# Two parked loads on another queue, and the returns of a norm tied behind the ways out

## The chip, the cores and the metric

The kernel runs on one core of one Trainium2 chip. The metric is the device time of one execution in microseconds; a lower number is better. Times of the kernel before are given as the median of three runs, and one further execution was taken with the hardware profiler.

## The reference

The program is a two-layer decoder trunk on 256 tokens of width 2048 in float32. Layer 0 mixes with gated linear attention, layer 1 with softmax attention that has a forget gate; both also attend to 256 memory tokens. Each layer ends in a gated MLP with a causal convolution of width 3. What matters here is the passage from layer 0 to layer 1:

```python
x = x + conv_ffn(rmsnorm(x, norm_ffn[0]), ...)        # end of layer 0
hs = rmsnorm(x, fox_kv_norm)                          # "kv" norm
k, v, fl = split_cols(hs @ fox_w_kv, [1536, 1536, 12])   # K and V of layer 1
mk, mv = memory_kv(mem_n, mem_w_kv[1])                # keys and values of the memory, layer 1
h = rmsnorm(x, norm_mix[1])                           # input of the queries of layer 1
```

So K and V of layer 1 need the whole of x after the last down projection of layer 0, normalised. The memory's keys and values of layer 1 don't depend on x, and they are first read when layer 1 attends to the memory.

## The kernel before

**Matrix products.** Every product is split into high and low float32r halves, and three of the four partial products are kept. A weight is streamed in units of at most 128 x 1024 (`raw`, four buffers), loaded on SP's queue (L224). ScalarE makes its high half (`whi`, L229) and VectorE its low half (`wlo`, L230), four buffers each. A panel of 512 columns that takes tokens as its rows (`panel_tm`, matmuls at L333) has eight units of two 128-row chunks, and 12 matmuls a unit: two chunks, two token blocks, high x high, high x low and low x high.

**The order of the work.** A planner fills each engine's queue from the order in which the program states things and from priorities (`high_priority`). Each engine then works through its own queue in that order; an instruction that waits holds all that stands behind it on the same engine, DMA issues included. `tc.issue_after(ins)` puts the instructions of its block behind `ins` where they share an engine, and adds no wait. The list `loads` holds the weight loads.

**Turning the residual.** x stands with tokens on partitions and is needed with features on partitions. A block `f` (0 to 3) is 512 features of all 256 tokens. For each block the norm's `then(f, b)` (in `preparing`) transposes 32 x 32 pieces on VectorE for both token halves `b` (L1592, into `blk` or `tblk`). After the second half, `far_away` sends the block to DRAM (the way out, L632, 512 KB, into `far`, three buffers). Later `land` calls `back`, which brings it back in four loads of 128 KB in another order (the return, L637, into `fvt` for blocks 0 to 2 and `fky` for block 3). Then `take` (`split_turned`, L524 on ScalarE for the high half, L526 on VectorE for the low half) scales it into `B` (chunks 4f to 4f+3), the input of K and V. The queries' input is made from the same block by the same two lines (`query_input`, out-tiles `mix` and `A`). For the "kv" norm at the end of layer 0 these transfers are issued by GpSimd (`queue=nc.gpsimd`); for the norms "ffn0" and "ffn1" they are issued by SP. In the MLP of layer 0, other blocks (`yu`) take the same way out and back on GpSimd.

**The end of layer 0.** The last down projections run as `wide` (blocks 0 and 1), `f2` (block 2) and `f3` (block 3). The program states `land()` of block 0 after unit 4 of `f2`, of block 1 after unit 5, of block 2 before unit 5 of `f3`; block 3 is landed inside layer 1's second K panel. Then `fox` starts with the K panels 0 and 1: six units of panel 0, six of panel 1, then the last two of each.

**Parked memory.** Layer 1's memory keys and values (`mk[1]`, `mv[1]`, 512 KB each) are computed early. The MLP of layer 0 needs their room for the hidden activations (`moremk`, `moremv`), so both are written to DRAM before it (`parked`, on GpSimd) and loaded back once the last matmul that reads the room is done (L1203, `mk1again` and `mv1again`). The program states that load in `fox`, in the second of four V panels after its fourth unit. They are read by `mem_parts(1, "B")` (L668, L669) after the last V panel.

Of the kernel before, what the change touches and what calls it, by code (L numbers as in the profile page):

```python
# [21 lines left out]
T = 256  # L22
# [123 lines left out]
def _trunk(ctx: ExitStack, tc: tile.TileContext, xt, xtok, memt, wp, wgu, gns, gfin, cnv, par, msk, out):  # L146
    nc = tc.nc
# [37 lines left out]
        for i in range(WARM):  # L185
            TE.matmul(warm, bufB[KC - 1][:, 0, :P], bufB[KC - 1], start=i == 0, stop=i == WARM - 1)

    loads, casts, lows, ends, last_mm = [], [], [], [], []
    scratch = [sm]
    parked = []  # L190

# [120 lines left out]
    def panel_tm(key, src, evac, second=False):  # L312

        units = where[key]
        n = units[0][2]
        base = min(min(u[1]) for u in units)
        acc = []
        end = len(units) - 1  # L320

        def step(i):
            if i == 0:
                acc.extend(work("s", 2) if second else pacc.tile([P, 512], F32, name="acc", tag="acc")
                           for _ in range(2))
            ready = split_unit(units[i])
            passes = [(b, low) for low in range(2) for b in range(2)]
            if i == end:
                passes.sort()
            for b, low in passes:  # L330
                for j, kc in enumerate(units[i][1]):
                    for part in range(2 - low):
                        mm = TE.matmul(acc[b][:, :n], src[kc - base][:, part, b * P : (b + 1) * P],  # L333
                                       ready[low][:, j * n : (j + 1) * n], start=i == low == part == j == 0,
                                       stop=i == end and low == 1 and j == len(units[i][1]) - 1)
                if i == end and low:
                    ends.append(mm)
                    evac(b, acc[b][:, :n])
            last_mm.append(mm)

        return step
# [177 lines left out]
    def split_turned(dst, i, z, name):  # L519

        g = gain(name, i)
        hi, lo = (dst[i][:, part, :].rearrange("p (b q j) -> p b q j", b=2, q=4) for part in range(2))
        src = z[:, :, i % 4].rearrange("p q b j -> p b q j")
        S.activation(hi, src, AF.Copy, scale=g)  # L524
        for b in range(2):
            V.scalar_tensor_tensor(lo[:, b], src[:, b], g, hi[:, b].bitcast(F32), ALU.mult, ALU.subtract)  # L526
# [102 lines left out]
    def far_away(pool, src, n, queue=nc.sync):  # L629

        far = pool.tile([P, 4 * T], F32, name="far", tag="far", bufs=3)
        queue.dma_start(far[:, : 4 * n], src[:, : 4 * n])  # L632
        blocks = far[:, : 4 * n].rearrange("(q i) (c n) -> c i q n", q=4, c=4)

        def back(dst):
            for c in range(4):
                queue.dma_start(dst[32 * c : 32 * (c + 1), : 4 * n].rearrange("i (q n) -> i q n", q=4), blocks[c])  # L637

        return back

    def move_far(pool, dst, src, n):
        far_away(pool, src, n)(dst)

    def flat(t):
        return t.rearrange("p c k b j -> p (c k b j)")
# [8 lines left out]
    def turn_out(y, done):  # L654

        def evac(b, a):
            with tc.high_priority(offset=AHEAD):
                V.transpose(y[:, :, :, b, :], a.rearrange("p (k c i) -> p c k i", c=4, i=32))
            if b:
                done(far_away(dram, flat(y), T))  # L660

        return evac
# [468 lines left out]
    def fox(nx, vt, stash):  # L1131
        hk, hq, mix = bufB, bufA, bufB
        with (
# [16 lines left out]
            def keys():  # L1150
                j, back, z = open_.pop(0)
                with tc.issue_after(loads[-1].ins):
                    back(flat(z))
                with tc.issue_after(lows[-1].ins):
                    for k in range(4):
                        V.tensor_tensor(by_run(kt[:, 4 * j + k, :]), z[:, :, k], by_run(nx.row()), ALU.mult)

            def query_input(i):
                split_turned(hq, i, (*stash, spare[1])[i // 4], "mix1")
# [11 lines left out]
            def forget():  # L1171
                fl = turn()
                bias = part[:, C_BF : C_BF + 1]
                e = fp.tile([P, T], F32, name="fe", tag="tmp", bufs=5)
                S.activation(e, fl, AF.Abs, bias=bias)
                S.activation(e, e, AF.Exp, scale=-1.0)
                S.activation(e, e, AF.Ln, bias=1.0)
                mz = fp.tile([P, T], F32, name="fm", tag="tmp", bufs=5)
                V.tensor_scalar(mz, fl, bias, 0.0, ALU.add, ALU.min)
                V.tensor_tensor(mz, mz, e, ALU.subtract)  # L1180
                V.tensor_tensor_scan(cs, ones[:, 0:1].to_broadcast([P, T]), mz, 0.0, ALU.mult, ALU.add)
                pc = work("t")
                for b in range(2):
                    TE.transpose(pc[:, b * P : (b + 1) * P], cs[:, b * P : (b + 1) * P], ident)
                V.tensor_copy(cc, pc[:, :T].rearrange("p (b h) -> p b h", b=2)[:, :, :FOX_H])

            for j, (lo, hi) in enumerate(FV_PARTS):
                def fv_out(b, a, j=j, lo=lo, hi=hi):
                    S.activation(vt[:, b, lo:hi], a[:, : hi - lo], AF.Copy, scale=nx.col()[:, b : b + 1])
                    if j == 0:  # L1190
                        take(b, a[:, hi - lo :])
                        if b:
                            forget()

                step = panel_tm(("fv", j), hk, fv_out)
                for u in range(8):
                    step(u)
                    if (j, u) in ((0, 0), (0, 2), (1, 2)):
                        keys()
                    if (j, u) == (1, 3):  # L1200
                        for t, tag, far in ((mk, "mk1", parked[0]), (mv, "mv1", parked[1])):
                            t[1] = const.tile(list(t[1].shape), F32, name=tag + "again", tag=tag)
                            nc.gpsimd.dma_start(t[1].rearrange("p a b -> p (a b)"), far)  # L1203
                    if j == 0:
                        query_input(4 + u)

# [31 lines left out]
            def take(pair, head):  # L1238

                def evac(c, a):  # L1240
                    if c == 0 and pair >= BEHIND:
                        values(pair - BEHIND)
                    head(c, a)
                    if c:
                        move_far(dp, zs[pair % 3], ys[pair % 2], T if pair < 2 else 6 * 32)

                proj_fm(("mq", 1, pair) if pair < 2 else ("fq", pair - 2), hq, evac)
# [312 lines left out]
    def preparing(name, dst, pool, far, kept=None, tag="blk", queue=nc.sync):  # L1560

        n = StreamNorm()
        blocks, rooms, turned_blocks = {}, {}, []
        away, landed = [], []

        def land(z=None):  # L1570

            f, back = away.pop(0)
            if z is None:
                z = pool.tile([P, 4, 4, 2, 32], F32, name="turn", tag="turn", bufs=2) if kept is None else kept[f]
            with tc.issue_after(loads[-1].ins) if queue is nc.sync else nullcontext():
                back(flat(z))
            landed.append((f, z))

        def take():

            f, z = landed.pop(0)
            with tc.issue_after(casts[-1].ins):
                for k in range(4):
                    split_turned(dst, 4 * f + k, z, name)

        def then(f, b):
            n.add(f, b)
            with tc.high_priority(offset=AHEAD):
                if b == 0:
                    blocks[f] = rooms[f]() if f in rooms else pool.tile([P, 4, 4, 2, 32], F32, name="blk", tag=tag, bufs=2)  # L1590
                y = blocks[f]
                turned_blocks.append(V.transpose(y[:, :, :, b, :],  # L1592
                                                 x[f][:, b, :].rearrange("p (k c i) -> p c k i", c=4, i=32)))
                if b:
                    away.append((f, far_away(far, flat(y), T, queue)))

        n.rooms = then.rooms = rooms
        then.turned = turned_blocks
        n.land = then.land = land
        n.take = then.take = take  # L1600
        return n, then

    n = gla(nx)
# [20 lines left out]
    with tc.tile_pool(name="turn2", bufs=1) as tp:  # L1624
        n, then = preparing("ffn1", bufA, tp, dram)
# [137 lines left out]
```

## Time and profile before

| | us |
|---|---|
| median of 3 runs | 2244.25 |
| lowest, highest | 2242.79, 2245.59 |
| the profiled execution | 2243.66 |
| its span, first to last instruction | 2241.9 |

| engine | busy us | share of the span |
|---|---|---|
| TensorE, matmuls (PE) | 2216.0 | 99% |
| TensorE, weight loads (PEld) | 1855.5 | 83% |
| VectorE (DVE) | 1781.2 | 79% |
| ScalarE (ACT) | 1419.2 | 63% |
| GpSimd (POOL) | 137.1 | 6% |

The busy time of TensorE counts a matmul from its start to its modelled end; matmuls overlap, and a matmul that runs at a lower clock or follows the one before it late is busy all the same. So a share of 99% doesn't say that no time is lost. The profile names who ended each engine's idle time, gives the granted clock of TensorE in any stretch (1.00 is full), and the time from the issue of a DMA to its landing. Rows that begin with a number have the start in microseconds from the span's start. In DMA rows POOLq is GpSimd's queue and SPq is SP's; in SP's and GpSimd's timelines the length of a DMA row is that of its issue, not that of the transfer.

### The profile page before, as it was taken

The numbers are of one execution on the slowest core, as the hardware profiler recorded it, in microseconds if no ns is written. First come the engines' busy times: TensorE is split into PE (matmuls) and PEld (weight loads), VectorE is DVE, ScalarE is ACT, GpSimd is POOL, SyncE is SP. The second block draws the span as 40 slices with busy tenths as digits, with TensorE's granted clock in tenths as the row PEclk, the third lists the DMA queues.
The fourth block names the chain that finished last, engine by engine and source line by source line (L and its number), as shares of the span: only waits on it lengthen the run. The fifth ranks groups of instructions, "written<-read, shape, count | busy, mean of one in ns | idle before, by whom it ended". The sixth has DMA issues, their size and how long they took to land.

```text
span 2241.9 us, 30033 instructions
## 1 busy us (share of the span) xinstructions
PE 2216.0 (99%) x10323; PEld 1855.5 (83%) x10323; DVE 1781.2 (79%) x2638; ACT 1419.2 (63%) x2255; POOL 137.1 (6%) x259
## 2 busy tenths in 40 slices
PE   9999999999999999999989999999999999999998
PEld 7888888888788888888877998888878888888886
DVE  7768987688887889888867559768888788978876
ACT  6655665556886567674665455455788647676466
POOL 0000000001100001100111000000100000110010
PEclk9999999999999999999999999999999999999999
DMA  9867657877677667766776767777777757776674
GB/s 352 248 220 222 199 183 248 247 243 240 217 245 243 206 215 253 230 213 220 226 244 225 221 197 233 241 235 242 224 230 243 244 197 229 257 233 209 224 239 158
DMA packets 165633, 515.47 MB, mean 230 GB/s; under 512 B 20700, under 2 KB 41832, under 8 KB 165480
## 3 DMA queue, kind: packets, MB, share of 16 engines
q1 hardware_dynamic: 148200, 460.32, 63.4%
q0 software_dynamic: 16704, 52.44, 7.6%
q8 instruction: 81, 1.33, 0.2%
q10 hardware_dynamic: 576, 0.79, 0.1%
q14 instruction: 72, 0.59, 0.1%
HBM read 469.68 MB, written 43.79 MB: 229 GB/s over the span
## 4 chain that ended last, share of the span: by engine, by line
PE 83%; issue 7%; ACT 4%; DMA 3%; DVE 1%; POOL 1%; ACTq 0%; DVEq 0%; POOLq 0%
PE acc L400 25%; PE acc L333 23%; PE ps_s L400 12%; PE ps_o L400 6%; PE ps_t L400 6%; PE acc L305 3%; PE acc L260 3%; PE ps_s L333 2%; ACT tap L1379 2%; PE acc L258 1%; ACT whi L229 1%; DMA raw<-wp 1%; DMA yzu<-far 1%; DMA far<-tblk 1%; DMA fvt<-far 1%
## 5 line engine op out<-in xcount | busy, mean ns | idle before, releaser
L230 DVE TENSOR_TENSOR wlo<-raw,whi 128x1024 fp32r<-128x1024 f32 (+4 forms) x739 | 875.6, 1196 | 305.0 <-ACT whi L229 287.8
L229 ACT ACTIVATE whi<-raw 128x1024 fp32r<-128x1024 f32 (+4 forms) x739 | 761.4, 1037 | 454.2 <-PE acc L333 171.7
L333 PE MATMUL acc<-whi,B 128*128 128x512 f32 (+3 forms) x1248 | 296.9, 373 | 10.9 <-ACT B L524 8.5
L333 PEld LDWEIGHTS acc<-whi,B 128*128 128x128 f32 x1248 | 229.2, 190 | 40.7 <-ACT B L524 9.3
L375 ACT ACTIVATE whi<-raw 128x1024 fp32r<-128x1024 f32 (+1 forms) x136 | 129.9, 955 | 196.3 <-PE acc L400 71.8
L400 PE MATMUL acc<-whi,B 128*128 128x512 f32 x794 | 203.3, 390 | 1.5 <-ACT whi L229 1.3
L376 DVE TENSOR_TENSOR wlo<-raw,whi 128x1024 fp32r<-128x1024 f32 (+1 forms) x136 | 148.1, 1090 | 69.3 <-ACT whi L375 61.7
L400 PE MATMUL acc<-whi,mix 128*128 128x512 f32 x754 | 192.7, 390 | 1.3 <-ACT whi L229 1.1
L400 PEld LDWEIGHTS acc<-whi,B 128*128 128x128 f32 x794 | 148.6, 188 | 34.6 <-ACT whi L229 3.8
L400 PEld LDWEIGHTS acc<-whi,mix 128*128 128x128 f32 x754 | 141.3, 188 | 32.7 <-ACT whi L229 3.0
L333 PE MATMUL acc<-wlo,B 128*128 128x512 f32 (+3 forms) x624 | 160.9, 371 | 0.0
L1379 ACT ACTIVATE tap<-fvt,cw 128x256 f32<-128x256 f32 x264 | 124.4, 530 | 6.9 <-DMA fvt<-far 6.9
L333 PEld LDWEIGHTS acc<-wlo,B 128*128 128x128 f32 x624 | 115.5, 189 | 14.9
L1379 ACT ACTIVATE tap<-yzu,cw 128x256 f32<-128x256 f32 x264 | 124.6, 531 | 4.7 <-DMA yzu<-far 4.7
L1386 DVE TENSOR_TENSOR tap<-tap,tap 128x1024 f32<-128x1024 f32 x88 | 107.0, 1216 | 19.6 <-ACT tap L1379 19.6
L400 PE MATMUL acc<-wlo,B 128*128 128x512 f32 x397 | 112.4, 390 | 0.0
L400 PE MATMUL ps_s<-whi,mix 128*128 128x512 f32 x394 | 107.3, 390 | 0.0
L400 PE MATMUL acc<-wlo,mix 128*128 128x512 f32 x377 | 106.6, 390 | 0.0
L400 PE MATMUL ps_s<-whi,B 128*128 128x512 f32 x342 | 94.3, 390 | 0.0
L400 PEld LDWEIGHTS acc<-wlo,B 128*128 128x128 f32 x397 | 74.4, 188 | 15.9 <-DVE wlo L230 0.5
L400 PEld LDWEIGHTS ps_s<-whi,mix 128*128 128x128 f32 x394 | 74.0, 188 | 15.6
L400 PEld LDWEIGHTS acc<-wlo,mix 128*128 128x128 f32 x377 | 70.6, 188 | 15.2 <-DVE wlo L230 0.5
(492 smaller groups left out, 3759.9 us busy)
## 6 DMA issues: line engine op xcount, KB each, us to landing
raw<-wp SPq DMA_DIRECT2D x743, 512.0 KB, 4.6
fvt<-far POOLq DMA_DIRECT2D x100, 128.0 KB, 5.2
raw<-wp SPq DMA_DIRECT2D x32, 384.0 KB, 3.5
far<-yu POOLq DMA_DIRECT2D x22, 512.0 KB, 5.8
far<-yzu POOLq DMA_DIRECT2D x22, 512.0 KB, 5.8
yzu<-far POOLq DMA_DIRECT2D x88, 128.0 KB, 5.6
raw<-wp SPq DMA_DIRECT2D x24, 388.0 KB, 3.5
x<-xtok SPq DMA_DIRECT2D x8, 512.0 KB, 6.3
```

Source lines behind the costliest of these rows:

```text
L229: casts.append(S.activation(hi[:, s], raw[:, s], AF.Copy))
L230: lows.append(V.tensor_tensor(lo[:, s], raw[:, s], hi[:, s].bitcast(F32), ALU.subtract))
L258: mm = TE.matmul(acc[p][c][:, :T], w[:, s], both[:, 0, :], start=False, stop=end and j == 3)
L260: mm = TE.matmul(acc[p][c], w[:, s], both, start=u == j == 0, stop=end and j == 3)
L305: mm = TE.matmul(acc[b][:, :n], src[kcs[j] - base][:, part, b * P : (b + 1) * P], w, start=u == 0 and low == part == j == 0, stop=u == end ...
L333: mm = TE.matmul(acc[b][:, :n], src[kc - base][:, part, b * P : (b + 1) * P], ready[low][:, j * n : (j + 1) * n], start=i == low == part = ...
L375: casts.append(S.activation(hi[:, :n], src, AF.Copy))
L376: lows.append(V.tensor_tensor(lo[:, :n], src, hi[:, :n].bitcast(F32), ALU.subtract))
L400: r = TE.matmul(bank[name], x, w, start=name not in begun, stop=last)
L1379: S.activation(by_run(taps[i][:, s, c, i:]), zs[slot][:, :, 2 * c + s], AF.Copy if i else AF.Identity, bias=0.0 if i else w[3], scale=w[2 ...
L1386: V.tensor_tensor(taps[0], taps[0], taps[n][:, :, :, :T], ALU.add)
```

## The change

The two loads of the parked memory are issued by SP instead of GpSimd, and they stand behind the weight load that was stated last at that place of the program (a load of the second V panel). `far_away` keeps each way out and the last load of each return in a new list `sent`. For the norm whose transfers GpSimd issues, a return stands behind the last entry of `sent`, and so does a way out. In the order of the program this puts the return of block 0 behind the way out of block 1, the way out of block 2 behind the return of block 0, the return of block 1 behind the way out of block 2, the return of block 2 behind that of block 1, and the way out of block 3 behind the return of block 2.

```diff
-    loads, casts, lows, ends, last_mm = [], [], [], [], []
+    loads, casts, lows, ends, last_mm, sent = [], [], [], [], [], []
 ...
     def far_away(pool, src, n, queue=nc.sync):
 
         far = pool.tile([P, 4 * T], F32, name="far", tag="far", bufs=3)
-        queue.dma_start(far[:, : 4 * n], src[:, : 4 * n])
+        sent.append(queue.dma_start(far[:, : 4 * n], src[:, : 4 * n]))
         blocks = far[:, : 4 * n].rearrange("(q i) (c n) -> c i q n", q=4, c=4)
 
         def back(dst):
             for c in range(4):
-                queue.dma_start(dst[32 * c : 32 * (c + 1), : 4 * n].rearrange("i (q n) -> i q n", q=4), blocks[c])
+                last_one = queue.dma_start(dst[32 * c : 32 * (c + 1), : 4 * n].rearrange("i (q n) -> i q n", q=4), blocks[c])
+            sent.append(last_one)
 
         return back
 ...
                     if (j, u) == (1, 3):
                         for t, tag, far in ((mk, "mk1", parked[0]), (mv, "mv1", parked[1])):
                             t[1] = const.tile(list(t[1].shape), F32, name=tag + "again", tag=tag)
-                            nc.gpsimd.dma_start(t[1].rearrange("p a b -> p (a b)"), far)
+                            with tc.issue_after(loads[-1].ins):
+                                nc.sync.dma_start(t[1].rearrange("p a b -> p (a b)"), far)
 ...
-            with tc.issue_after(loads[-1].ins) if queue is nc.sync else nullcontext():
+            with tc.issue_after((loads if queue is nc.sync else sent)[-1].ins):
                 back(flat(z))
 ...
                 if b:
-                    away.append((f, far_away(far, flat(y), T, queue)))
+                    with tc.issue_after(sent[-1].ins) if queue is nc.gpsimd else nullcontext():
+                        away.append((f, far_away(far, flat(y), T, queue)))
```

## The prediction

> **What bounds the kernel now.** I read the page's head first, then the table of waits for TensorE, then the timelines of the engines around the waits it names, then the granted clock there, and last the landing times of the transfers.
>
> ```profile
> span 2241.9 us, 30033 instructions
> PE 2216.0 (99%) x10323; PEld 1855.5 (83%) x10323; DVE 1781.2 (79%) x2638; ACT 1419.2 (63%) x2255; POOL 137.1 (6%) x259
> ```
> The profiled execution took 2243.66 us, 1.8 outside its span and 0.6 under the median of the three runs. TensorE has work for 99% of the span, so only a place where TensorE stands still or runs slowly can give time back. Its largest waits, here from the stretch 1160 to 1260 (engine, line, waited for: us in total, times, longest):
>
> ```profile
> PE acc L333 <- ACT B L524: 8.5, 2, 7.4
> PE acc L333 <- DVE B L526: 2.4, 1, 2.4
> ```
> Both are one place: the first K panel of the second layer waits for its normalised input B. TensorE's timeline there (start, us, instruction, count, idle before it and who ended it):
>
> ```profile
> 1169.46 1.07 PE L333 MATMUL acc<-wlo,mix 128*128 128x512 f32 x4
> 1177.93 3.35 PE L333 MATMUL acc<-whi,B 128*128 128x512 f32 x7 [7.40 <-ACT B L524]
> ...
> 1187.64 0.73 PE L333 MATMUL acc<-whi,B 128*128 128x512 f32 x2 [1.08 <-ACT B L524]
> 1190.75 2.41 PE L333 MATMUL acc<-whi,B 128*128 128x512 f32 x5 [2.38 <-DVE B L526]
> ...
> 1203.21 1.98 PE L333 MATMUL ps_s<-whi,B 128*128 128x512 f32 x8
> 1205.02 1.07 PE L333 MATMUL ps_s<-wlo,B 128*128 128x512 f32 x4
> ```
> Eight matmuls step in 1205.02 - 1203.21 = 1.81 us, 0.227 each. The down projection's last four therefore end their turn at 1170.37. Until 1203.21, where the second K panel begins, there stand six weight units of 12 matmuls (72, 16.32 us) and two of half width (0.23): 16.55 us of work in 32.84 us. **The place loses 16.3 us.** Part of it is the clock (stretch, its length, TensorE's busy us and count, granted clock, DMA share, GB/s):
>
> ```profile
> 1177.93:1184.05 6.12, 6.12 (x14) 0.50 1.01 384
> 1190.75:1194.30 3.55, 3.55 (x9) 0.52 0.66 173
> ```
> After the long gap TensorE works at half clock (6.12 x 0.50 = 3.1 us lost), and again after the second pair of gaps (3.55 x 0.48 = 1.7). The gaps are 7.56 and 3.78 (1.08 + 2.38; each 0.16 more than its row says, since the rows let a matmul end 0.16 after its turn: 1169.46 + 1.07 against 1170.37). Gaps and clock, 4.8, make 16.1 of the 16.3.
>
> What ends the first gap is ScalarE, which itself waits for the return of block 0 of the turned residual, and GpSimd's queue says why that return is late:
>
> ```profile
> 1170.89 0.42 ACT L608 ACTIVATE sq<-x 128x256 f32<-128x256 f32 x1 [0.18 <-DVE x L483]
> 1177.37 1.70 ACT L524 ACTIVATE B<-fvt,gains 128x256 fp32r<-128x256 f32 x4 [5.97 <-DMA fvt<-far]
> ```
> ```profile
> 1158.96 0.56 POOL L632 DMA_DIRECT2D far<-blk  x1 [29.02 <-DVE blk L1592]
> 1165.25 0.57 POOL L1203 DMA_DIRECT2D mk1again<-parkmk  x1 [5.73 <-PE acc L333]
> 1165.88 2.21 POOL L637 DMA_DIRECT2D fvt<-far  x4
> 1168.08 0.56 POOL L632 DMA_DIRECT2D far<-blk  x1
> 1168.63 0.57 POOL L1203 DMA_DIRECT2D mv1again<-parkmv  x1
> 1169.19 0.53 POOL L632 DMA_DIRECT2D far<-tblk  x1
> 1174.36 0.53 POOL L632 DMA_DIRECT2D far<-tblk  x1 [4.64 <-DMA mk1again<-parkmk]
> 1180.24 2.21 POOL L637 DMA_DIRECT2D fvt<-far  x4 [5.35 <-DMA far<-blk]
> 1183.53 2.18 POOL L637 DMA_DIRECT2D fvt<-far  x4 [1.07 <-DMA far<-tblk]
> ```
> The parked keys (L1203) stand in GpSimd's queue ahead of block 0's return and wait 5.73 us for matmuls that still read the room they go to; the return and block 1's way out stand behind. Then two 512 KB parked loads share the engines with the returns:
>
> ```profile
> far<-blk POOLq DMA_DIRECT2D x1, 512.0 KB, 4.2
> ```
> ```profile
> fvt<-far POOLq DMA_DIRECT2D x4, 128.0 KB, 9.4
> ```
> ```profile
> mv1again<-parkmv POOLq DMA_DIRECT2D x1, 512.0 KB, 13.5
> ```
> ```profile
> DMA to landing us min/median/max: 2.8/5.2/9.7
> ```
> ```profile
> far<-yu POOLq DMA_DIRECT2D x22, 512.0 KB, 5.8
> ```
> These are block 0's way out, its return (median of four), the parked values, all returns into fvt, and the ways out of the MLP before it.
>
> **The change, part by part.** *Parked loads away from GpSimd.* Two issues of 0.57 leave GpSimd. In the changed program's order, GpSimd then has: out 0, out 1, return 0, out 2, returns 1 and 2, out 3, return 3. So each tie puts a return behind the next block's way out, and whatever is late there holds all behind it. Only VectorE's transposes can hold these:
>
> ```profile
> 1161.48 0.70 DVE L1592 STREAM_TRANSPOSE blk<-x 128x512 f32<-128x512 f32 x1
> 1165.53 0.71 DVE L1592 STREAM_TRANSPOSE tblk<-x 128x512 f32<-128x512 f32 x1
> ...
> 1171.31 1.22 DVE L230 TENSOR_TENSOR wlo<-raw,whi 128x1024 fp32r<-128x1024 f32 x1
> 1172.45 1.30 DVE L1592 STREAM_TRANSPOSE tblk<-x 128x512 f32<-128x512 f32 x2
> 1177.91 2.19 DVE L526 SCALAR_TENSOR_TENSOR B<-fvt,gains,B 128x128 fp32r<-128x128 f32 x8 [4.16 <-ACT B L524]
> ```
> Out 1 can go at 1162.2 (was 1168.08) and is issued by 1162.8. Block 0's way out lands at 1158.96 + 4.2 = 1163.2, so return 0 is issued from 1163.2 to 1165.4 (was 1165.88 to 1168.09). Its last quarter starts at 1164.85 and lands at 1167.6 to 1174.5 by the least and the greatest landing, at 1170.0 by the median, which I take: without the parked loads it is like the other returns.
>
> *First gap.* ScalarE is busy with the square until 1171.3, then splits B; TensorE's first two matmuls (high halves) start about 1171.8. The third needs a low half from VectorE, whose queue has the weight's low half and the last transposes first, until 1173.7; two low halves of 0.27 more make it 1174.3. That holds for every landing up to 1173.4. Lost: 1174.3 - 1170.37 - 0.45 = 3.5 us in two pieces (1.4, 2.1), against 7.56.
>
> *Later blocks.* Out 2 goes at 1166.3, return 1 when block 1's way out is there (1162.2 + 5.8 = 1168.0), issued to 1170.2, landed 1175 (at the greatest 1179.4). TensorE needs it 22 matmuls after 1174.3, at 1179.3. Return 2: 1166.3 + 5.8 = 1172.1, landed 1179 to 1184, needed 1185. Out 3 goes about 1174.5, return 3 about 1180.3, landed by 1187 to 1192; its halves on VectorE stand ahead of a weight's low half that TensorE reaches at about 1200. So no transfer is late; VectorE is next. In its queue, from 1173.7: eight halves of B 2.1, eight of the query input 2.1, one weight 1.2, then block 1's first pair 0.55: 1179.7 to 1179.9, where TensorE, two high matmuls into the block, wants it at 1179.75. The same again for block 2. I give both together 0.4 us, against 3.78.
>
> *Clock.* The lost 3.5 us lie within 3.9. In the old trace gaps of 1.08 and 2.38 with two matmuls between were followed by the clock of 0.52 above. So I count one such drop, 1.7 us, with 0 and 3.4 (two of its length) as ends. The Trainium skill's page "TensorE: Matmul & The Clock Gate", section "Why this matters for your kernels", asks only that no gap be longer than about 3 us; by it neither piece would drop the clock, and the time would be 1.7 less. The two measured gaps, both shorter than that and yet followed by 0.52, differ from the rule, and the trace decides.
>
> *Parked loads on SP.* They follow the first load of the second V panel: two issues on SP, behind them seven value loads.
>
> ```profile
> 1265.00:1275.00 10.00, 10.00 (x59) 9.93 (x58) 6.32 (x10) 5.79 (x11) 0.00 (x0) 1.00 0.76 233
> ```
> ```profile
> raw<-wp SPq DMA_DIRECT2D x1, 388.0 KB, 6.3
> ```
> ```profile
> ACT whi L229 <- DMA raw<-wp: 1.5, 1, 1.5
> ```
> ```profile
> 1305.89 0.61 ACT L668 ACTIVATE kv<-mk1again 128x512 fp32r<-128x512 f32 x1
> ```
> There 233 GB/s move where 384 did above: 1.05 MB extra takes 2.7 us of the engines at 384, 6.9 us of what is free. At about 1283 a value load took 6.3 us; ScalarE waited 1.5 and no row has TensorE waiting. ScalarE splits each weight four units ahead (one unit is 12 matmuls of 388 columns, 12 x 0.227 x 388/512 = 2.1 us), so TensorE starts to lose when a load takes over 6.3 - 1.5 + 3 x 2.1 - 0.85 = 10.3 us. I take nothing, with 0 to 3 us as bounds (13.5, the slowest landing above, less 10.3). The keys are read at 1305.89, some 25 us after the slowest landing seen, counted from 1266. The last steps of the norm's root move later on VectorE and ScalarE; their reader is the key scaling in the V panel, and the weight splits between hide them. A gain is not to be had here, since no wait of TensorE stands here to be taken away.
>
> **Sum.** Lost before 16.3; after 3.5 + 0.4 + 1.7 = 5.6. Gain 10.7 us, from 2243.66 to 2233.0 as profiled, **2233.5 us** as a median. With the clock kept whole 2231.8; with the greatest landing (low half 1.3 later) and two clock lengths 2236.5.
>
> **Rivals.** *The clock stays whole.* Two pieces of 1.4 and 2.1 us are too little for a drop: 2231.8. For it: two drops are all that the trace has to judge by, and one of them followed 7.4 us. Against it: the pair of 1.08 and 2.38 was no longer. 0.20.
> *The room is taken by others.* Value loads, out 1 and out 2 still share the engines with return 0, and it lands at 1177.3 as before. For it: the engines' share of 1.01 above. Then only the second pair of gaps and its clock goes, 3.78 + 1.7: 2238.8. The Trainium skill's page "DMA: Bandwidth & Descriptors", section "Issuing engines are not separate DMA queues", says the same of a change of queue: all issuers use the same 16 engines, and another queue saves issue time alone. Against it: the parked bytes move by 100 us, not only by queue. 0.15.
> *Nothing is won.* Returns 0 and 1 both come as late as before, since ties replace the waits: return 0 behind out 1, return 1 behind out 2. 2244. Against it: the rows have both transposes done by 1166.3. 0.08.
> *The value loads starve.* On SP's one queue seven value loads stand behind both parked loads. Each microsecond over 10.3 stops TensorE, and two lengths of half clock add 3.4. It decides against the change when a load takes over 10.3 + 10.7 - 3.4 = 17.6 us. Were both parked loads to land one after the other at 13.5 each, the load behind would land at 27: 16.7 + 3.4 lost, 2253.6. For it: 13.5 was seen. Against it: that was with five other transfers of 512 KB on the way. 0.05.
>
> **How the numbers follow.** The forecast with its drop of the clock has 0.52 (2232.5 to 2236.5), the whole clock 0.20. The range, 2229.5 to 2239.5, holds both and most of the rival at 2238.8; below it goes 2.3 under 2231.8, 1.4 for the spread of the three runs (2242.79 to 2245.59) and the rest for the 0.4 of small waits and the 0.3 of the loss that the rows leave unexplained. 0.2% is 4.5 us, about what a measurement of this kernel can tell from no change. Faster by more (under 2239.8): the forecast, the whole clock and three quarters of the rival at 2238.8, 0.83. Within: the rest of that rival and the one at 2244, 0.12. Slower: 0.05.
>
> **What would show it.** Right: return 0 issued about 1163 and landed by 1173; TensorE's wait on B at L524 in pieces of 1 to 2.5 us in place of 7.4; the second K panel begins near 1192; no wait of TensorE between 1255 and 1310. Wrong: a gap of over 5 us before the first K panel, half clock for over 7 us there, or TensorE waiting on a weight in the V panels.

## The result and the profile after

The changed kernel takes 2235.48 us (median of 6 runs, 2234.6 to 2236.24); the kernel before 2243.8 (median of 6, the three runs from above and three more, 2242.79 to 2248.14). The ratio is 0.996 with a 95% interval of 0.9947 to 0.9972: **faster by 8.3 us**, where 10.7 were forecast. The profiled execution took 2235.35 us. Its page begins:

```profile
span 2233.6 us, 30036 instructions
...
PE 2212.0 (99%) x10323; PEld 1852.3 (83%) x10323; DVE 1779.7 (80%) x2638; ACT 1418.3 (63%) x2255; POOL 136.1 (6%) x257
```

In the table of TensorE's waits over the same stretch, the wait on VectorE has gone and those on ScalarE's B are smaller:

```profile
PE acc L333 <- ACT B L524: 5.7, 2, 4.8
```

TensorE's timeline from the last down matmuls to the second K panel, whose first unit now stands ahead of the last six matmuls of the first:

```profile
1170.37 1.07 PE L333 MATMUL acc<-wlo,mix 128*128 128x512 f32 x4
1176.22 3.30 PE L333 MATMUL acc<-whi,B 128*128 128x512 f32 x7 [4.78 <-ACT B L524]
...
1184.28 1.89 PE L333 MATMUL acc<-whi,B 128*128 128x512 f32 x7 [0.90 <-ACT B L524]
...
1193.99 1.98 PE L333 MATMUL ps_s<-whi,B 128*128 128x512 f32 x8
...
1197.17 1.07 PE L333 MATMUL ps_s<-wlo,B 128*128 128x512 f32 x4
```

The last down matmuls end their turn at 1170.37 + 4 x 0.227 = 1171.28, 0.91 later than in the trace before (a wait of 1.1 for a weight, earlier than all this). From there to 1197.17 are 25.89 us, with 16.55 of work in the first panel and 8 x 0.227 = 1.81 in the unit that stands ahead: **7.5 us are lost, against 16.3 before.** The gaps are 4.94 and 1.06, and one drop of the clock is left of two (stretch, length, TensorE's busy us, its granted clock, DMA share, GB/s):

```profile
1175.91:1179.32 3.41, 3.10 (x7) 2.48 (x8) 3.12 (x12) 3.41 (x12) 0.27 (x1) 0.50 1.05 335
```

GpSimd's queue, without the parked loads:

```profile
1159.87 0.56 POOL L632 DMA_DIRECT2D far<-blk  x1 [28.96 <-DVE blk L1594]
1165.97 0.56 POOL L632 DMA_DIRECT2D far<-blk  x1 [5.54 <-DVE wlo L230]
1166.60 2.21 POOL L637 DMA_DIRECT2D fvt<-far  x4
1168.81 0.56 POOL L632 DMA_DIRECT2D far<-tblk  x1
1171.07 0.56 POOL L637 DMA_DIRECT2D fvt<-far  x1 [1.70 <-DMA far<-blk]
...
1179.05 2.17 POOL L637 DMA_DIRECT2D fvt<-far  x4 [5.28 <-DMA far<-tblk]
```

The transposes of block 1, for which the second line waits, had ended at 1162.39 + 0.70 = 1163.09 (VectorE's timeline):

```profile
1162.39 0.70 DVE L1594 STREAM_TRANSPOSE blk<-x 128x512 f32<-128x512 f32 x1
```

So way out 1 went 2.9 us behind its last input, where way out 0 and others go 0.3 behind theirs. That is the new thing in this trace. The returns then take long; these are the DMA issues of return 0 and of return 1 (median from issue to landing):

```profile
fvt<-far POOLq DMA_DIRECT2D x4, 128.0 KB, 6.6
```
```profile
fvt<-far POOLq DMA_DIRECT2D x4, 128.0 KB, 9.4
```

From 1170 to 1185 the 16 DMA engines are full, a share of 1.03:

```profile
1170.00:1185.00 15.00, 9.32 (x34) 6.98 (x33) 10.22 (x28) 8.41 (x22) 4.92 (x9) 0.89 1.03 312
```

Return 0's last quarter lands at 1175.55, return 1's at 1183.56, each right ahead of the matmuls that wait for it. The parked loads went on SP at 1256.0 and 1256.5; TensorE waits for nothing from 1210 to 1320, and the keys are read from 1298.3.

### The profile page after: what moved, and what is told of

Read it like the earlier page. It is cut to its first block, busy times and chain, and to the rows that moved or that the text cites. A ratio compares the mean times of both kernels' runs of the same rounds, so it can differ in the third digit from the quotient of the medians.

```text
span 2233.6 us, 30036 instructions
## 1 busy us (share of the span) xinstructions
PE 2212.0 (99%) x10323; PEld 1852.3 (83%) x10323; DVE 1779.7 (80%) x2638; ACT 1418.3 (63%) x2255; POOL 136.1 (6%) x257
## 4 chain that ended last, share of the span: by engine, by line
PE 91%; ACT 3%; issue 2%; DMA 2%; DVE 0%; POOL 0%; SPq 0%; ACTq 0%; DVEq 0%; POOLq 0%
PE acc L400 27%; PE acc L333 23%; PE ps_s L400 14%; PE ps_o L400 7%; PE ps_t L400 7%; PE acc L305 3%; PE acc L260 3%; PE ps_s L333 2%; DMA fvt<-far 2%; PE acc L258 1%; ACT tap L1381 1%; ACT whi L229 1%; PE acc L361 1%; PE ps_s L1008 0%; ACT whi L375 0%
```

## Experiments

A run's total wanders by 1 to 2 us in places that these edits do not touch, so each trace was also read over one stretch: from the start of the last down matmul (before: 1169.46 + 3 x 0.227 = 1170.14) to the forget gate's first transpose. Before and after:

```profile
1281.43 0.38 PE L1184 MATMUL ps_t<-mask,fc 128*128 128x128 f32 x2
```
```profile
1273.84 0.38 PE L1185 MATMUL ps_t<-mask,fc 128*128 128x128 f32 x2
```

That gives 111.3 and 102.8 us; of the 8.3 between the spans, 8.5 are this stretch, -0.9 lies ahead of it and 0.7 behind. All kernels (median, number of runs, ratio to the kernel before run beside it with its 95% interval, then the two ends and the length of the stretch):

| kernel | us (n) | ratio | from | to | stretch |
|---|---|---|---|---|---|
| before | 2243.8 (6) | 1 | 1170.14 | 1281.43 | 111.3 |
| after | 2235.48 (6) | 0.996 (0.9947-0.9972) | 1171.05 | 1273.84 | 102.8 |
| queue_alone | 2238.1 (7) | 0.9972 (0.9961-0.9983) | 1169.37 | 1274.69 | 105.3 |
| ties_alone | 2241.11 (11) | 0.9991 (0.9982-1.0) | 1168.99 | 1278.63 | 109.6 |
| shift40 | 2236.61 (5) | 0.9964 (0.9952-0.9977) | 1170.78 | 1274.17 | 103.4 |
| shift128 | 2235.25 (5) | 0.9959 (0.9946-0.9971) | 1169.54 | 1272.92 | 103.4 |
| after_four | 2243.9 (11) | 1.0 (0.9991-1.0009) | 1181.90 | 1284.96 | 103.1 |
| before_four | 2249.03 (11) | 1.0021 (1.0012-1.003) | 1178.25 | 1285.34 | 107.1 |
| queue_four | 2243.24 (11) | 0.9999 (0.999-1.0007) | 1177.59 | 1280.58 | 103.0 |
| kv_sync | 2235.59 (4) | 0.9962 (0.9948-0.9976) | 1169.04 | 1270.59 | 101.6 |
| after_mid | 2236.51 (5) | 0.9964 (0.995-0.9978) | 1171.90 | 1273.42 | 101.5 |
| after_bytes | 2236.96 (5) | 0.9964 (0.9951-0.9976) | 1169.69 | 1273.68 | 104.0 |
| after_warm | 2235.4 (5) | 0.9959 (0.9946-0.9971) | 1170.90 | 1273.58 | 102.7 |
| bytes_later | 2236.85 (8) | 0.997 (0.9959-0.9981) | 1169.41 | 1274.64 | 105.2 |

After, shift40 and shift128 are the same program in the stretch: 102.8, 103.4, 103.4. Differences under 0.7 are not read, and each stretch is one trace.

**The two parts alone.** queue_alone:

```diff
-                            nc.gpsimd.dma_start(t[1]..., far)      # parked loads; no ties on GpSimd
+                            with tc.issue_after(loads[-1].ins):
+                                nc.sync.dma_start(t[1]..., far)
```

> The kernel before with one part of the change: the two parked loads go to SP behind the last load of values, and no tie is added on GpSimd. GpSimd's order becomes way out 0, return 0, way out 1, way out 2, return 1, way out 3, return 2, return 3. If the parked loads in GpSimd's queue and their 1 MB in the DMA engines are the whole loss, about the changed kernel's time: 2235 to 2237 us, return 0 landing at 1172 to 1175. If the ties carry half of the gain: 2239 to 2241 us. If the ties hurt (return 0 need not stand behind way out 1): 2232 to 2234.

ties_alone is the changed kernel with this one edit taken back.

> The changed kernel with its other part alone: the ties stay, the parked loads are back on GpSimd (the first stands between way out 0 and way out 1, the second behind return 0). If the parked loads are the whole loss: 2241 to 2244 us, as before. If the order of ways out and returns is worth half of it: 2238 to 2240.

Measured: 2238.1, between the first two forecasts, and 2241.11, at the lower end of the first; the stretch falls by 6.0 and by 1.7, by 8.5 with both. The interval of ties_alone reaches 1.0, so the ties without the move are barely clear of no change. The move off GpSimd is the larger part, and with it done the ties give 2.5 more. GpSimd's timeline of queue_alone shows what they alter:

```profile
1158.19 0.56 POOL L632 DMA_DIRECT2D far<-blk  x1 [29.18 <-DVE blk L1593]
1165.19 2.19 POOL L637 DMA_DIRECT2D fvt<-far  x4 [6.45 <-ACT whi L229]
1167.38 0.56 POOL L632 DMA_DIRECT2D far<-blk  x1
...
1176.77 0.57 POOL L637 DMA_DIRECT2D fvt<-far  x1 [8.28 <-DMA far<-blk]
```

Here return 0, ahead of way out 1, is what starts 7 us behind way out 0, and way out 1 comes behind it at 1167.38; return 1 waits 8.28 for way out 1 to land and goes at 1176.77, against 1171.07 in the changed kernel. That looks like the cost, and is not: its quarters take only 3.6 to 3.9 us there instead of 9 to 10.3, and counted from the start of the last down matmul it lands 12.9 us later, in the changed kernel 12.5. What makes up the 2.5 us is smaller things: block 0 begins 0.5 later (5.70 us behind the last down matmul, 5.17 in the changed kernel), 13 matmuls run at half clock instead of 7 (about 1.2 more lost), and ahead of and in block 1 TensorE stands 1.87 us (1.25 and 0.62) instead of 1.06. ScalarE's split for block 1 stands there behind a weight's high half and not behind return 1.

```profile
1173.68:1180.51 6.83, 5.44 (x13) 4.28 (x14) 4.96 (x18) 5.25 (x17) 2.77 (x5) 0.50 0.99 363
```

**What holds GpSimd behind way out 0?** In the traces of before and after GpSimd's second instruction starts 6.1 to 6.3 us behind way out 0, whatever it is. In before it is the first parked load, and the matmuls that read its room end at 1161.30 + 1.07 = 1162.37, 2.9 us ahead of it, so there too the named releaser had long ended:

```profile
1161.30 1.07 PE L333 MATMUL acc<-wlo,moremk 128*128 128x512 f32 x4
```

First theory: code that has to be fetched. shift40 and shift128:

```diff
-    nc.gpsimd.memset(eps, EPS)
+    for _ in range(41):                      # shift128: range(129)
+        nc.gpsimd.memset(eps, EPS)
```

> The changed kernel with 40 more one-element-wide memsets of eps on GpSimd in the first microseconds, where GpSimd is idle for 80 us. They only move the place in GpSimd's code at which each later instruction stands. In both kernels GpSimd's second instruction behind way out 0 starts 6.1 to 6.3 us after it, though in the changed one its transposes had ended 2.9 us earlier; an 8 KB instruction packet runs 2.7 us behind way out 0 in both. If GpSimd waits there for code: the hold moves elsewhere, way out 1 goes 0.3 us behind its transpose (1163.4), return 0 lands 2 to 3 us sooner (1172.5 to 1173.5), and the time is 2232 to 2234 us. If GpSimd is held by VectorE's unbroken work, or by the way out itself: way out 1 stays at 1166, and 2235 to 2236 us.

> The same with 128 more memsets, 8 KB of GpSimd's code at 64 B each. If GpSimd waits for code that comes in pieces of 8 KB: the hold is back at the same place, way out 1 at 1166, and the time is the changed kernel's, 2235 to 2236 us. If it waits for something else that 40 memsets disturb, no reason that it comes back; if VectorE or the way out holds it, it never went.

Measured: 2236.61 and 2235.25, and the hold stays where it was, in shift40:

```profile
1159.60 0.56 POOL L633 DMA_DIRECT2D far<-blk  x1 [29.51 <-DVE blk L1595]
1165.71 0.56 POOL L633 DMA_DIRECT2D far<-blk  x1 [5.55 <-DVE wlo L231]
```

Two 8 KB instruction packets did move with 40 memsets (607 to 464 us, 1175.7 to 958), but the one near way out 0 (1162.6, in shift40 1162.3) did not, so nothing links it to GpSimd's code. In shift128 way out 1 goes 6.1 us behind way out 0 as well. **The theory fell.** What the traces share is the DMA's number: GpSimd's 114th DMA is held in all of them, and so is its 220th (counted from 1; the expectations below count from 0). In the changed kernel, the 220th is the second quarter of a return (the four quarters elsewhere stand 0.55 apart), in before a way out whose transpose had ended at 2003.58:

```profile
2005.49 0.56 POOL L637 DMA_DIRECT2D yzu<-far  x1 [8.64 <-ACT whi L229]
2008.51 1.63 POOL L637 DMA_DIRECT2D yzu<-far  x3 [2.47 <-issue]
```
```profile
2006.46 0.56 POOL L632 DMA_DIRECT2D far<-yzu  x1 [3.38 <-DVE wlo L230]
```

So four DMAs more, ahead of all others, should bring the hold to the gate's last returns. after_four, before_four and queue_four (the last on queue_alone):

```diff
     nc.gpsimd.memset(eps, EPS)
+    idle = dram.tile([P, 4], F32, name="idle")
+    for i in range(4):
+        nc.gpsimd.dma_start(idle[:, i : i + 1], eps)
```

> The changed kernel with four more DMAs on GpSimd at the very start, each of 128 x 4 bytes to a place that nothing reads. The hold of way out 1 did not move with 40 or 128 more memsets, so it is not code. In all six traces it sits at the same ordinal: GpSimd's DMA number 113 (counted from 0) starts 2.6 us later than its last input plus 0.3 us allows, and so does number 219, whatever these two are (way out 1, a parked load or a return). Theory, bookkeeping of GpSimd's DMA queue: with four DMAs more the hold falls on the gate's last four returns, which have 29 us of slack; way out 1 goes 0.3 us behind its transpose, 3.5 to 3.8 us behind way out 0 instead of 6.1, return 0 is issued some 2.5 us sooner and lands 2 to 3 us sooner, TensorE's first wait of 4.8 to 5.3 us shrinks to 2 to 3, and the time is 2232 to 2233.5 us. Rival, VectorE's unbroken work holds GpSimd there: way out 1 still 6.1 us behind way out 0, 2235 to 2236 us.

> The kernel before with the same four DMAs. By the theory of the DMA's number: the first parked load goes 3 to 3.7 us behind way out 0 instead of 6.3, return 0 lands 1 to 2.6 us sooner, and 2241 to 2243 us; the rest of the loss stays, since the parked loads still stand in the queue. By the rival: 6.3 us again and 2244 us.

> The parked loads on SP without the ties on GpSimd, and the same four DMAs: what the ties are worth when the hold is gone. Return 0 stands ahead of way out 1 and need only wait for way out 0 to land (some 3.6 us): issued from 1162, landed at 1168 to 1170. If the tie of return 0 behind way out 1 costs what it looks like on paper: 2230 to 2232 us, faster than the changed kernel with four. If the ways out are what must go first (the later returns hang on them): 2233 to 2236 us.

The totals missed all three forecasts by 5 to 12 us, because four DMAs of 4-byte rows at the start cost 7 us or more there (last section). The stretch, one trace each, shows what was asked: before falls by 4.2, to 107.1, the changed kernel stays (103.1), where the theory had it faster, and with the hold gone the ties are worth nothing: 103.0 without them. And in before_four the wait of the first parked load, 5.73 us in before, is 2.3:

```profile
POOL mk1again L1206 <- PE acc L336: 2.3, 1, 2.3
```

after_mid moves the hold without that cost:

```diff
                         away = far_away(dram, flat(y), T, nc.gpsimd)
+                        if l == 0 and j == 8:
+                            idle = dram.tile([P, 512], F32, name="idle")
+                            for i in range(4):
+                                nc.gpsimd.dma_start(idle[:, P * i : P * (i + 1)], flat(y)[:, :P])
```

> The changed kernel with four more DMAs on GpSimd of 64 KB each, to a place that nothing reads, now in the first gate at about 550 us (at the very start, four DMAs of 128 x 4 bytes cost 8 us by themselves before the first 100 us were over, which hid what they were to show). The hold of 2.5 us then falls on one of the gate's last returns; way out 1 goes 0.3 us behind its transpose and return 0 when way out 0 has landed, some 3.7 us behind it. If return 0's moment is what the first wait hangs on: return 0 lands 2 us sooner and the time is 2233 to 2234 us. If the DMA engines' room is (their share stands at 1.01 to 1.03 from 1170 to 1185 us): the wait goes over to the next returns and the time is 2235 to 2236.

```profile
1127.90 0.56 POOL L637 DMA_DIRECT2D fvt<-far  x1 [8.25 <-ACT tap L1381]
1130.93 1.64 POOL L637 DMA_DIRECT2D fvt<-far  x3 [2.47 <-issue]
1160.82 0.56 POOL L632 DMA_DIRECT2D far<-blk  x1 [28.25 <-DVE blk L1598]
1164.34 0.56 POOL L632 DMA_DIRECT2D far<-blk  x1 [2.96 <-DVE blk L1598]
1165.58 2.30 POOL L637 DMA_DIRECT2D fvt<-far  x4 [0.68 <-ACT sq L608]
```

The hold (2.47) now stands inside the gate's last return, on the 114th DMA; way out 1 goes 3.5 us behind way out 0 instead of 6.1, 0.3 behind its transpose. VectorE does the same transposes and low halves around it in both traces, so its work is not what held way out 1. Return 0 and return 1 are issued 2 to 3.5 us sooner, counted from way out 0, but return 1 now takes 11.2 (median of its quarters) against 9.4:

```profile
fvt<-far POOLq DMA_DIRECT2D x4, 128.0 KB, 11.2
```

The stretch gains 1.3 us; the total, 2236.51, gains nothing (the place behind the stretch took 1.9 more in this trace, which I can't tell from its ordinary spread). So the second expectation is the nearer one (0.5 above it), but not by the way it names: no wait at block 1 stands in this trace. Return 1, issued 3 to 3.5 us sooner, lands 1.2 sooner, counted from the last down matmul (11.3 us against 12.5), and block 1 begins 1.2 sooner; that is the stretch's gain.

**What do the parked loads' bytes cost?** after_bytes and bytes_later put 1 MB back, out of GpSimd's queue (as stores to DRAM, where the parked loads read from it):

```diff
                         away.append((f, far_away(far, flat(y), T, queue)))
+                    if name == "kv" and f in (1, 2):       # bytes_later: f == 2, twice, on nc.scalar, no tie
+                        again = dram.tile([P, 4 * T], F32, name="again", tag="again", bufs=2)
+                        with tc.issue_after(loads[-1].ins):
+                            nc.sync.dma_start(again, x[f].rearrange("p b t -> p (b t)"))
```

> The changed kernel with two more ways out of 512 KB each on SP (x blocks 1 and 2 to a place that nothing reads), at the time when before had its parked loads on GpSimd: the same 1 MB of 4 KB rows in the same stretch, but in no one's way on GpSimd's queue. If the parked loads cost by their bytes: 1 MB at the 310 to 340 GB/s of that stretch is 3.1 to 3.4 us, so 2238 to 2240 us. If they cost by their places in GpSimd's queue: 2235 to 2236 us.

> The changed kernel with 1 MB more, now nearer to the moment at which before had its parked loads (1165.3 and 1168.6): x block 2 goes twice to a place that nothing reads, from ScalarE's queue, at about 1164 to 1165 us. With the same MB on SP at 1158.8 and 1162.3 the stretch from the last down matmul to the forget gate's transpose was 104.0 us, against 102.8 in the changed kernel (103.4 in two kernels that are the same there) and 105.3 with the parked loads on SP but no ties; before has 111.3. If the bytes are the loss, and only came too early there: 106 to 108 us for the stretch and 2238.5 to 2241 for the whole. If they are worth about 1 us wherever they stand, and the rest of the loss was the places in GpSimd's queue: 103.5 to 105 for the stretch and 2236 to 2237.5 for the whole.

They were issued at 1158.8 and 1162.3, and in bytes_later at 1162.1 and 1162.4, sooner than expected. 2236.96 and 2236.85; the stretch is 104.0 and 105.2, so 1 MB costs 0.6 to 2.4 us, the lower end too small to be read; after_bytes lies between its two forecasts, bytes_later within the one for the places in the queue, its stretch 0.2 above. The time goes into return 0, whose quarters take 9.7 (median) in bytes_later against 6.6, and TensorE's one wait is 8.0 us:

```profile
fvt<-far POOLq DMA_DIRECT2D x4, 128.0 KB, 9.7
```

No run had the bytes at 1165 to 1169, where before has them; there they may cost more. By these two, 3.6 to 5.4 of the 6.0 us of queue_alone are the loads' places in GpSimd's queue, which is a difference and not a measurement of its own.

**Is the half clock worth its 1.7 us?** after_warm:

```diff
             open_ = []
 
+            with tc.issue_after(last_mm[-1].ins):
+                warm2 = work("o")
+                for i in range(16):
+                    TE.matmul(warm2, more[0][:, 0, 0, :P], more[0][:, 0], start=i == 0, stop=i == 15)
```

> The changed kernel with 16 matmuls more on TensorE behind the last down matmul (their result is not read): 16 x 0.227 = 3.6 us of the gap of 4.9 us in which TensorE waits for return 0. If the stretch at half clock behind that gap (3.41 us at 0.5, up to 1.7 us lost) comes from the gap's length: it goes, and the time falls by 1 to 1.7 us, to 2234 to 2234.5. If it comes in any case: no change, 2235 to 2236. If return 0 would have come sooner than 3.6 us in some runs: slower by up to 1 us.

```profile
1171.13 3.79 PE L1149 MATMUL ps_o<-moremk 128*128 128x512 f32 x16
1176.63 1.87 PE L333 MATMUL acc<-whi,B 128*128 128x512 f32 x7 [1.71 <-ACT B L524]
...
1184.04 1.88 PE L333 MATMUL acc<-whi,B 128*128 128x512 f32 x7 [1.69 <-ACT B L524]
```
```profile
1174.76:1184.04 9.28, 5.88 (x25) 4.43 (x24) 5.69 (x20) 6.01 (x17) 2.73 (x5) 1.00 1.03 305
```

The granted clock stays 1.00 with the gap cut from 4.94 to 1.87 us, and nothing is won: 2235.4 us, stretch 102.7. The second block begins 13.1 us behind the last down matmul's start (1184.04 - 1170.90), 13.2 in the changed kernel (1184.28 - 1171.05): what the clock gave back became a longer wait for return 1 (1.69 against 0.90). That holds for a drop as short as this one. In shift40 and shift128, the same program here, half clock lasts twice as long, TensorE comes to block 1 without any wait for it, and the stretch is 0.6 longer in both, just less than is read here. shift40:

```profile
1175.71:1182.54 6.83, 6.21 (x15) 4.86 (x16) 4.39 (x18) 5.55 (x15) 2.73 (x5) 0.50 1.05 299
```

**All on SP.** kv_sync:

```diff
-            n2, then = preparing("kv", bufB, tp, dram, turned3, "raw2", nc.gpsimd)
+            n2, then = preparing("kv", bufB, tp, dram, turned3, "raw2")
```

> The changed kernel with all ways out and returns of this norm on SP, among the weight loads, as the other norms have theirs. If GpSimd's hold is what is left of the loss: 2231 to 2234 us. If the weight loads that then stand on SP behind ways out (each waiting for its transposes) come late for the K panels: 2237 to 2245 us.

2235.59 us, between the two forecasts, stretch 101.6. TensorE goes into block 0 without a gap and then waits once, for block 1:

```profile
1169.27 1.86 PE L333 MATMUL acc<-whi,B 128*128 128x512 f32 x7
...
1178.39 3.35 PE L333 MATMUL acc<-whi,B 128*128 128x512 f32 x7 [3.40 <-ACT B L524]
```

GpSimd's hold is out of the way, return 0 is early, and the wait moves to the next block. Block 1 begins 9.35 us behind the last down matmul's start, 3.9 sooner than in the changed kernel, but the stretch gains only 1.2. Behind this wait the clock does count: 14 matmuls run at half clock for 5.80 us, by estimate 2.9 us lost where the changed kernel loses nothing any more. No run fills this gap.

```profile
1177.37:1184.19 6.82, 5.80 (x14) 4.54 (x15) 6.70 (x22) 6.36 (x15) 0.00 (x0) 0.50 1.07 300
```

No kernel here beats the changed one by more than its spread.

## Why the forecast was right, and where it was not

The total came within its range and the gain was 8.3 of 10.7 us, but of the signs that the prediction named only one came plainly, that TensorE waits for nothing from 1255 to 1310. Return 0 was issued at 1166.60 and landed at 1175.55 (about 1163 and by 1173 were named), the first wait was 4.78 in one piece (1 to 2.5 were named), and the second K panel began at 1193.99 (near 1192 was named), though its first unit stands ahead of the first panel's last matmuls. The sign against it, a gap of over 5 us, missed this trace by 0.06 and stands in shift40 (5.32) and shift128 (5.44). So the hit owes something to luck and to the width of the range.

**Parked loads away from GpSimd: right** in order and sign. The first loss went from 7.56 to 4.94, the second from 3.78 to 1.06, and one clock drop of two went. The sum was 5.6 us of loss; 7.5 were measured (before: 16.3).

**"Only VectorE's transposes can hold these": wrong.** Out 1 was to go at 1162.2 (1163.1 with this trace's 0.91) and went at 1165.97. GpSimd's 114th DMA is held for some 2.5 us, and that was way out 1. The same hold was in the trace before: 5.73 us of wait for the parked keys, which I put down to matmuls alone as the row says. The matmuls had ended 2.9 us ahead of that load. before_four has 2.3 for the matmuls' part, and a stretch 4.2 us shorter than before's with the hold elsewhere.

**Return 0: late by its bounds.** Issued 1166.6 to 1168.8 instead of 1164.1 to 1166.3 (the forecast and 0.91), landed at 1175.55, just behind the forecast's last value (1174.5 + 0.91). So the gap was 4.94 in one piece and not 3.5 in two.

**"So no transfer is late; VectorE is next": wrong, and this is the mis-sized term.** Return 1 was to land at 1175, by 1179.4 at the latest; it landed at 1183.56. Its issue was 3 us late (way out 1 again), and its transfer took 9 to 10.3 us where I took 5.2 from the median of returns. The transfer weighs more: in after_mid an issue 3 us sooner brought the landing 1.2 sooner, and in queue_alone one 7.4 us later cost 0.4. From 1171.28 to 1184.28, where block 1 begins, are 13.0 us with 24 matmuls, 5.45: the whole loss of 7.5 us lies there. In this trace the gaps and the clock that I added up are parts of one wait for return 1. kv_sync and after_mid bear it out from the other side: in kv_sync return 0 is early and TensorE waits at block 1 alone, in after_mid block 1 begins as much sooner as return 1 lands. shift40, with no wait at block 1, shows that the wait has little to spare.

**The clock: right in size in this trace, wrong in worth.** One drop of 3.41 us at 0.50, as forecast; that it was one length is luck, since shift40 and shift128 have two. after_warm takes it away and wins nothing. On the rule of the Trainium skill's page "TensorE: Matmul & The Clock Gate", section "Why this matters for your kernels" (no gap longer than about 3 us): behind 4.94 us the clock fell, with pieces of 1.87 and 1.85 in after_warm it did not, so these runs agree with it; the drop behind 1.08 and 2.38 in the trace before stays outside it. before_four has another such: behind a gap of 2.30 us and two matmuls the clock falls to 0.50 at 1181.20 for 6.83 us. In queue_four gaps of 1.20 and 1.30 with two matmuls between have no drop behind them.

**Parked loads on SP: right.** No wait of TensorE, as taken.

**The rivals.** *The room is taken by others* was nearer than its 0.15 said: return 0 landed at 1175.55 and not at 1177.3, but returns 0 and 1 took 6.6 and 9.4 us with the engines' share at 1.03, 1 MB more made return 0 take 9.7 (bytes_later), and issuing them sooner (after_mid) or from another queue (kv_sync) did not make the kernel faster. That the full engines set these times is the likeliest reading, not a separate measurement. The Trainium skill's page "DMA: Bandwidth & Descriptors", section "Issuing engines are not separate DMA queues", says of a change of queue that it saves issue time alone; kv_sync's total agrees. Its block 1 began 3.9 us sooner, more than the hold of 2.5 on GpSimd explains, and where the rest comes from no run shows. What the changed kernel won beside issue places are the bytes themselves, moved by 90 us, 0.6 to 2.4 us in two runs. *Nothing is won*, *the clock stays whole* and *the value loads starve* did not come.

Open: what GpSimd does in the held 2.5 us, why after_four gains nothing in the stretch by moving it, and why 1.2 us less in the stretch of after_mid and kv_sync does not show in their totals.

## What to carry to other kernels

Where several transfers in a row release one panel each, find the one whose landing lies furthest behind its due time and count the loss to there; the gaps, slow clocks and small waits ahead of it are not added as long as a wait for that landing is left, since time won there turns into a longer wait. Ahead of a transfer that must be early, move away both the issues in its queue and the bytes at its time, and try each alone: here the places were worth more than the bytes, by a difference of two runs. When an instruction starts late and its named releaser had long ended, compare the delay in other programs by ordinal, before explaining it by what happens to run beside it.

## What the hardware showed

- **GpSimd's 114th and 220th DMA start about 2.5 us late.** In all 13 traces in which this norm's DMAs are GpSimd's the 114th is late, as a way out, a return or a parked load; four DMAs more moved the place (to 1130.93 in after_mid), 40 or 128 memsets more did not. In kv_sync, where this norm's DMAs are SP's, the 114th is a way out of the next MLP, and it goes 2.9 us behind its transpose (1557.94 against 1555.06). The 220th is held by 2.4 to 2.6 us wherever it waits for nothing else.
- **Four DMAs of 128 rows of 4 bytes held up the start by 7.0 to 7.5 us.** By so much the first way out of the first MLP goes later in the three kernels with them (510.58 in after_four, 503.07 in the changed kernel), a little less than the 8 that the expectation of after_mid states. In after_four the third weight load takes 11.8 us to land, in the changed kernel 6.0, and TensorE's wait for a weight there is 6.00 us:

```profile
raw<-wp SPq DMA_DIRECT2D x1, 512.0 KB, 11.8
```
```profile
raw<-wp SPq DMA_DIRECT2D x1, 512.0 KB, 6.0
```
```profile
15.07 3.74 PE L308 MATMUL acc<-whi,A 128*128 128x512 f32 x8 [6.00 <-ACT whi L232]
```

Four of 64 KB in the middle of the first gate cost nothing that shows (after_mid 2236.51 us, the changed kernel 2235.48, with overlapping intervals).
